# Batched experts on one core: float32 weights over SyncE's ring, cast on chip, experts in strict order

## The chip, the core and the metric

The kernel runs on one core of one Trainium2 chip. A core has engines that run side by side, each with its own instruction queue worked off in order: TensorE (PE; its weight loads are shown as PEld), VectorE (DVE), ScalarE (ACT), GpSimd (POOL) and SyncE (SP). They meet only at semaphores. Sixteen DMA engines move data between the chip's main memory (HBM) and the core's SBUF (128 partitions); a transfer is issued from an engine's queue. In this kernel transfers are issued by GpSimd, which can convert the data type on the way, and by SyncE, whose transfers here copy bytes as they are. TensorE writes its results to PSUM, from where VectorE or ScalarE copy them to SBUF.

The metric is the device time in microseconds (us). The kernel before has a median of 181.65 us over three runs (181.58 to 182.18). The profile comes from one further execution, whose first to last instruction span 180.0 us.

## What is computed

```python
# x (8, 256, 512), w1 (8, 512, 2048), w2 (8, 2048, 512), all float32
h = np.matmul(x, w1)
h = np.maximum(h, 0)
return np.matmul(h, w2).astype(np.float32)
```

Eight experts, each with a first layer (x times w1, then relu) and a second layer (h times w2). Each w1 and each w2 is 4.194 MB of float32, x and the output are 4.194 MB each. Each weight is used once, so 71.30 MB have to be read and 4.19 MB written.

## The kernel before

All matmuls run in bf16. A weight is loaded by one transfer from GpSimd's queue (`load_w1`, L67, and `load_w2`, L71) that reads float32 and lands bf16 in a buffer of 16 KB per partition; there are three buffers for each kind of weight (`WB = 3`), so a load waits until the matmuls on the buffer three experts earlier are done. On each partition the rows of a weight are one contiguous stretch of 32 KB in HBM. The w2 of the last two experts comes in two pieces.

x is taken in four groups of 1, 1, 2 and 4 experts (`GROUPS`, L34). The first two land as float32 through SyncE (L145) and are cast by ScalarE (L155, L156); the other two land as bf16 through GpSimd's queue (L65). `transpose_x` (L77) transposes 128 x 128 blocks on TensorE (L87), and VectorE (L100) or ScalarE (L98) copies them from PSUM into `xt`. For groups of more than one expert that copy writes with a stride: every second bf16 element for the group of two, every fourth for the group of four.

`first_layer` (L102) takes 64 matmuls (L110) in four quarters of 16; each quarter fills one of two PSUM buffers and is followed by a relu into `ht`, on ScalarE (L120) for quarters 0 and 2 and on VectorE (L118) for quarters 1 and 3. Quarter q reads the columns q*4 to q*4+3 of every 16 columns of w1. `second_layer` (L124) takes 32 matmuls (L130) into two PSUM tiles, which VectorE (L137) and ScalarE (L138) copy to `o_sb`.

The order on each engine is written out by hand (`manual_schedule`, L48): the calls from L144 on are issued as they stand. Experts 0 to 4 run first and second layer in turn. For experts 5, 6 and 7 the three first layers come first (L185), then the three second layers (L191). Most of the output of experts 0 to 4 is stored through GpSimd's queue behind the last weights (L189, L190), a few rows of expert 0 through SyncE (L169), and experts 5 to 7 by one last store through SyncE (L193).

Of the kernel before, what the change touches and what calls it, by code (L numbers as in the profile page):

```python
# [9 lines left out]
@with_exitstack  # L10
def kernel(
    ctx: ExitStack,
    tc: tile.TileContext,
    x: bass.AP,
    w1: bass.AP,
    w2: bass.AP,
    out: bass.AP,
):
    nc = tc.nc
    P = 128  # L20
    bf = mybir.dt.bfloat16
    f32 = mybir.dt.float32
    relu = mybir.ActivationFunctionType.Relu

    E, C, H = x.shape
    F = w1.shape[2]
    MT = C // P
    KT1 = H // P
    KT2 = F // P
    FB = 4  # L30
    WB = 3


    GROUPS = ((0, 1), (1, 1), (2, 2), (4, 4))  # L34


    w1_r = w1.rearrange("e (p kt) n -> e p kt n", p=P)
    w2_r = w2.rearrange("e (p kt) n -> e p kt n", p=P)
    out_r = out.rearrange("e (p mt) n -> p e mt n", p=P)

    const = ctx.enter_context(tc.tile_pool(name="const", bufs=1))
    wpool = ctx.enter_context(tc.tile_pool(name="weights", bufs=WB))
    hpool = ctx.enter_context(tc.tile_pool(name="hidden", bufs=3))
    ps_h = ctx.enter_context(tc.tile_pool(name="ps_h", bufs=2, space=bass.MemoryType.PSUM))
    ps_o = ctx.enter_context(tc.tile_pool(name="ps_o", bufs=4, space=bass.MemoryType.PSUM))


    ctx.enter_context(tc.manual_schedule())  # L48

    w1_sb, w2_sb, ht = {}, {}, {}  # L50
    group_of = {e: g for g, (e0, n) in enumerate(GROUPS) for e in range(e0, e0 + n)}
    x_f = const.tile([P, 2, MT, H], f32, name="x_f")
    x_b = [const.tile([P, n * MT, H], bf, name=f"x_b{g}") for g, (_, n) in enumerate(GROUPS)]
    xt = [const.tile([P, KT1, MT, n * P], bf, name=f"xt{g}") for g, (_, n) in enumerate(GROUPS)]
    o_sb = const.tile([P, E, MT, H], f32, name="out_sb")
    identity = const.tile([P, P], bf, name="identity")

    def x_rows(g):
        e0, n = GROUPS[g]
        return x[e0:e0 + n].rearrange("e c k -> (e c) k").rearrange(  # L60
            "(p j) k -> p j k", p=P
        )

    def load_x(g):
        nc.gpsimd.dma_start(x_b[g][:], x_rows(g))  # L65

    def load_w1(e):  # L67
        w1_sb[e] = wpool.tile([P, KT1, F], bf, tag="w1", name="w1_sb")
        nc.gpsimd.dma_start(w1_sb[e][:], w1_r[e])  # L69

    def load_w2(e):  # L71
        w2_sb[e] = wpool.tile([P, KT2, H], bf, tag="w2", name="w2_sb")
        cuts = {E - 2: (0, 8, 16), E - 1: (0, 9, 16)}.get(e, (0, KT2))
        for lo, hi in zip(cuts, cuts[1:]):
            nc.gpsimd.dma_start(w2_sb[e][:, lo:hi, :], w2_r[e, :, lo:hi, :])  # L75

    def transpose_x(g, blocks=None):  # L77


        n = GROUPS[g][1]  # L80
        J = n * MT
        KB = 8 // J
        for b in blocks if blocks is not None else range(KT1 // KB):
            pt = ps_o.tile([P, KB, J, P], bf, tag="ps_o", name="pt_tr")
            for i in range(KB):
                for j in range(J):
                    nc.tensor.transpose(  # L87
                        pt[:, i, j, :], x_b[g][:, j, b * KB + i::KT1], identity[:]
                    )
            for i in range(KB) if n > 1 else (slice(0, KB),):  # L90
                if n > 1:
                    src = pt[:, i].rearrange("p (l m) q -> p l m q", m=MT)
                    dst = xt[g][:, b * KB + i].rearrange("p m (q l) -> p l m q", l=n)
                    flip = b * KB + i
                else:
                    src, dst, flip = pt[:, i], xt[g][:], g
                if flip % 2:
                    nc.scalar.copy(dst, src)  # L98
                else:
                    nc.vector.tensor_copy(dst, src)  # L100

    def first_layer(e, between=()):  # L102
        g = group_of[e]
        i0 = (e - GROUPS[g][0]) * P
        ht[e] = hpool.tile([P, KT2, C], bf, tag="ht", name="ht_sb")
        for q in range(KT2 // FB):
            ph = ps_h.tile([P, FB, C], f32, tag="ps_h", name="pt_h")
            for i in range(FB):
                for kt in range(KT1):
                    nc.tensor.matmul(  # L110
                        ph[:, i, :],
                        w1_sb[e][:, kt, FB * q + i::KT2],
                        xt[g][:, kt, :, i0:i0 + P],
                        start=(kt == 0),
                        stop=(kt == KT1 - 1),
                    )
            if q % 2:
                nc.vector.tensor_relu(ht[e][:, FB * q:FB * (q + 1), :], ph[:])  # L118
            else:
                nc.scalar.activation(ht[e][:, FB * q:FB * (q + 1), :], ph[:], relu)  # L120
            if between:
                between.pop(0)()

    def second_layer(e):  # L124
        po = [
            ps_o.tile([P, H], f32, tag="ps_o", name=f"pt_o{mt}") for mt in range(MT)
        ]
        for kt in range(KT2):
            for mt in range(MT):
                nc.tensor.matmul(  # L130
                    po[mt][:],
                    ht[e][:, kt, mt * P:(mt + 1) * P],
                    w2_sb[e][:, kt, :],
                    start=(kt == 0),
                    stop=(kt == KT2 - 1),
                )
        nc.vector.tensor_copy(o_sb[:, e, 0, :], po[0][:])  # L137
        nc.scalar.copy(o_sb[:, e, 1, :], po[1][:])  # L138

    def store(e0, e1):  # L140
        nc.gpsimd.dma_start(out_r[:, e0:e1], o_sb[:, e0:e1])  # L141


    for e in (0, 1):  # L144
        nc.sync.dma_start(x_f[:, e], x_rows(e))  # L145
    load_w1(0)
    make_identity(nc, identity)
    load_w2(0)
    load_x(2)
    load_w1(1)  # L150
    load_w2(1)
    load_x(3)
    load_w1(2)
    load_w2(2)
    nc.scalar.copy(x_b[0][:], x_f[:, 0])  # L155
    nc.scalar.copy(x_b[1][:], x_f[:, 1])  # L156
    transpose_x(0)

    first_layer(0)
    load_w1(3)  # L160
    transpose_x(1)
    second_layer(0)
    load_w2(3)
    first_layer(1)
    load_w1(4)
    transpose_x(2)
    second_layer(1)
    for p in range(112, P, 4):
        nc.sync.dma_start(out_r[p:p + 4, 0], o_sb[p:p + 4, 0])  # L169
    load_w2(4)  # L170
    first_layer(2, [lambda kt=kt: transpose_x(3, [kt]) for kt in range(KT1)])
    load_w1(5)
    second_layer(2)
    first_layer(3)
    load_w1(6)
    second_layer(3)
    first_layer(4)
    load_w1(7)
    load_w2(5)
    load_w2(6)  # L180
    second_layer(4)
    load_w2(7)


    for e in (5, 6, 7):  # L185
        first_layer(e)


    store(1, 5)  # L189
    nc.gpsimd.dma_start(out_r[:112, 0], o_sb[:112, 0])  # L190
    for e in (5, 6, 7):  # L191
        second_layer(e)
    nc.sync.dma_start(out_r[:, 5:8], o_sb[:, 5:8])  # L193


# [28 lines left out]
```

## Time and profile before

| | |
|---|---|
| Median of three runs | 181.65 us |
| Span of the profiled execution | 180.0 us |
| Instructions | 1823 |
| First-layer matmuls (L110) | 512, 67.6 us busy, 31.9 us idle before them, on weights |
| Second-layer matmuls (L130) | 249 recorded, 56.2 us busy, 7.9 us idle before them |
| relu on VectorE and ScalarE (L118, L120) | 16 each, 19.7 and 16.5 us busy |
| Weight transfers issued by GpSimd (L69, L75) | 18 |
| Granted TensorE clock, mean | 0.933 |

How to read the lines that follow. The page gives, for each engine, busy time, share of the span and number of instructions; then rows of 40 digits, one for each fortieth of the span, in tenths of busy time; then the DMA queues with their packets, megabytes landed and share of the 16 engines' time. The chain of waits goes back from the last instruction to what released each step. A group row has the line, engine and operation, what it writes and reads, partitions x elements, its count, then busy us and mean ns, then the idle time of the engine before it and what ended that. A row of the timeline has start, duration, engine and line, and in square brackets the idle time before it and its releaser. A row of stretches has the busy time of each engine in it (with counts), the granted TensorE clock, the busy share of the DMA engines and GB/s. A row of DMA issues has the size of a transfer in KB and the us from issue to landing.

### The profile page before, as it was taken

How to read it: one execution, taken by the hardware profiler on the slowest of the kernel's cores; microseconds unless marked ns; L12 is line 12 of the kernel's file. 1: busy time of each engine (PE TensorE's matmuls, PEld its weight loads, DVE VectorE, ACT ScalarE, POOL GpSimd, SP SyncE). 2: the span in 40 equal slices, each digit the busy share in tenths (PEclk: the TensorE clock that was granted, in tenths of full speed). 3: DMA queues.
4: the chain of work that ended last, by engine and by line, in shares of the span. 5: the costliest groups of instructions: out<-in, count | busy, mean ns of one | idle time of the engine just before them, and what ended most of it. 6: DMA issues, size and time to landing. Idle time of an engine off the chain costs nothing.

```text
span 180.0 us, 1823 instructions
## 1 busy us (share of the span) xinstructions
PE 127.5 (71%) x825; PEld 90.1 (50%) x832; DVE 31.8 (18%) x29; ACT 31.6 (18%) x32; POOL 12.7 (7%) x28
## 2 busy tenths in 40 slices
PE   0206999059993199987869497949895876997930
PEld 0105964048840189637723395428795873442410
DVE  0100220101411018610401022010423050101010
ACT  3300240102231026612200022012222220101010
POOL 7300010100101000100100004021010000000000
PEclk9999999957999659999999789996999999999995
DMA  5998998999999999999999999999999999999996
GB/s 210 256 226 182 233 229 178 233 211 215 200 244 204 222 218 208 218 215 229 204 222 218 218 211 211 229 208 222 215 222 208 215 215 204 224 213 209 334 411 248
DMA packets 4262, 40.47 MB, mean 225 GB/s; under 512 B 416, under 2 KB 416, under 8 KB 1952
## 3 DMA queue, kind: packets, MB, share of 16 engines
q0 software_dynamic: 3536, 37.68, 95.7%
q1 hardware_dynamic: 720, 2.69, 3.9%
q8 instruction: 6, 0.10, 0.2%
HBM read 71.30 MB, written 4.19 MB: 419 GB/s over the span
## 4 chain that ended last, share of the span: by engine, by line
DMA 45%; PE 40%; another core or an unknown queue 8%; POOL 1%; issue 1%; ACT 0%; POOLq 0%
DMA w_sb<-in_w_dram 45%; PE pt_o L130 19%; PE pt_h L110 19%; PE pt_tr L87 2%; POOL w_sb L69 0%; ACT out_sb L138 0%; POOL x_b L65 0%; POOL w_sb L75 0%; POOL identity masks.py:199 0%; POOL identity masks.py:197 0%; POOLq masks.py:199 0%; POOLq L208 0%
## 5 line engine op out<-in xcount | busy, mean ns | idle before, releaser
L110 PE MATMUL pt_h<-xt,w_sb 128*128 128x256 bf16 x512 | 67.6, 299 | 31.9 <-DMA w_sb<-in_w_dram 31.9
L110 PEld LDWEIGHTS <-w_sb 128*128 128x128 bf16 x512 | 60.9, 148 | 39.1 <-DMA w_sb<-in_w_dram 35.0
L130 PE MATMUL pt_o<-w_sb,ht_sb 128*128 128x512 bf16 x249 | 56.2, 379 | 7.9 <-DMA w_sb<-in_w_dram 7.4
L130 PEld LDWEIGHTS <-ht_sb 128*128 128x128 bf16 x256 | 24.9, 98 | 37.4 <-issue 7.2
L118 DVE TENSOR_SCALAR ht_sb<-pt_h 128x1024 bf16<-128x1024 f32 x16 | 19.7, 1229 | 69.3 <-PE pt_h L110 69.3
L120 ACT ACTIVATE ht_sb<-pt_h 128x1024 bf16<-128x1024 f32 x16 | 16.5, 1031 | 72.6 <-PE pt_h L110 72.6
L138 ACT COPY out_sb<-pt_o 128x512 f32<-128x512 f32 x8 | 4.7, 586 | 58.9 <-PE pt_o L130 58.9
L137 DVE COPY out_sb<-pt_o 128x512 f32<-128x512 f32 x8 | 5.5, 692 | 53.6 <-PE pt_o L130 53.6
L69 POOL DMA_DIRECT2D w_sb<-in_w_dram x8 | 4.4, 556 | 87.4 <-PE pt_h L110 86.6
L100 DVE COPY xt<-pt_tr 128x1024 bf16<-128x1024 bf16 (+1 forms) x5 | 7.1, 1449 | 18.2 <-PE pt_tr L87 18.2
L87 PE MATMUL pt_tr<-identity,x_b 128*128 128x128 bf16 x64 | 5.6, 242 | 5.3 <-ACT x_b L155 5.3
L98 ACT COPY xt<-pt_tr 128x1024 bf16<-128x1024 bf16 (+1 forms) x5 | 7.4, 1494 | 6.9 <-PE pt_tr L87 4.3
L87 PEld LDWEIGHTS <-x_b 128*128 128x128 bf16 x64 | 4.9, 121 | 5.4 <-ACT x_b L155 5.3
L75 POOL DMA_DIRECT2D w_sb<-in_w_dram x10 | 5.4, 547 | 20.3 <-PE pt_o L130 20.3
L155 ACT CAST x_b<-x_f 128x1024 bf16<-128x1024 f32 x1 | 1.0, 1045 | 2.1 <-DMA x_f<-in_x_dram 2.1
L155 ACT ACT_TABLE_LOAD x1 | 1.3, 1283 | 0.7 <-PEq L208 0.7
L190 POOL DMA_DIRECT2D out_dram<-out_sb x1 | 0.5, 545 | 8.6 <-DMA w_sb<-in_w_dram 8.6
L65 POOL DMA_DIRECT2D x_b<-in_x_dram x2 | 1.1, 550 | 0.0
L156 ACT CAST x_b<-x_f 128x1024 bf16<-128x1024 f32 x1 | 1.0, 1047 | 0.1
L141 POOL DMA_DIRECT2D out_dram<-out_sb x1 | 0.8, 768 | 1.8 <-DMA w_sb<-in_w_dram 1.8
masks.py:199 POOL TENSOR_SCALAR_AFFINE_SELECT identity<-identity 128x128 bf16<-128x128 bf16 x1 | 0.3, 288 | 0.1
masks.py:197 POOL MEMSET identity<- 128x128 bf16 x1 | 0.2, 225 | 0.0
(4 smaller groups left out, 0.4 us busy)
## 6 DMA issues: line engine op xcount, KB each, us to landing
w_sb<-in_w_dram POOLq DMA_DIRECT2D x14, 2048.0 KB, 45.4
w_sb<-in_w_dram POOLq DMA_DIRECT2D x2, 1024.0 KB, 45.4
out_dram<-out_sb POOLq DMA_DIRECT2D x1, 2048.0 KB, 53.0
out_dram<-out_sb SPq DMA_DIRECT2D x1, 1536.0 KB, 6.0
w_sb<-in_w_dram POOLq DMA_DIRECT2D x1, 1152.0 KB, 46.6
x_f<-in_x_dram SPq DMA_DIRECT2D x2, 512.0 KB, 3.7
x_b<-in_x_dram POOLq DMA_DIRECT2D x1, 1024.0 KB, 47.9
w_sb<-in_w_dram POOLq DMA_DIRECT2D x1, 896.0 KB, 50.3
```

The source lines that it names most:

```text
L69: nc.gpsimd.dma_start(w1_sb[e][:], w1_r[e])
L75: nc.gpsimd.dma_start(w2_sb[e][:, lo:hi, :], w2_r[e, :, lo:hi, :])
L87: nc.tensor.transpose(pt[:, i, j, :], x_b[g][:, j, b * KB + i::KT1], identity[:])
L98: nc.scalar.copy(dst, src)
L100: nc.vector.tensor_copy(dst, src)
L110: nc.tensor.matmul(ph[:, i, :], w1_sb[e][:, kt, FB * q + i::KT2], xt[g][:, kt, :, i0:i0 + P], start=(kt == 0), stop=(kt == KT1 - 1),)
L118: nc.vector.tensor_relu(ht[e][:, FB * q:FB * (q + 1), :], ph[:])
L120: nc.scalar.activation(ht[e][:, FB * q:FB * (q + 1), :], ph[:], relu)
L130: nc.tensor.matmul(po[mt][:], ht[e][:, kt, mt * P:(mt + 1) * P], w2_sb[e][:, kt, :], start=(kt == 0), stop=(kt == KT2 - 1),)
L137: nc.vector.tensor_copy(o_sb[:, e, 0, :], po[0][:])
L138: nc.scalar.copy(o_sb[:, e, 1, :], po[1][:])
L155: nc.scalar.copy(x_b[0][:], x_f[:, 0])
```

## The change

All transfers are issued by SyncE, and none converts. Weights and x land as float32 in a staging pool of three buffers of 32 KB per partition (`fpool`), used in turn by x, w1 and w2. VectorE and ScalarE cast each weight into one bf16 buffer for w1 and one for w2: `cast_w1` and `cast_w2` each make four chunks, half of a chunk on each engine, 1024 elements per partition on either. The chunks of w1 are the columns of one quarter; chunks 0 and 1 are issued ahead of the first matmul, chunk q+2 behind the matmuls of quarter q and ahead of that quarter's relu. The four chunks of w2 are issued ahead of the second layer's matmuls, behind the last relu. x is cast half on VectorE and half on ScalarE. `ht` has one buffer instead of three.

The experts run in strict order, first then second layer of each. x of experts 4 to 7 is cast and transposed between expert 1 and expert 2. Only the w2 of the last expert comes in two pieces. Experts 0 to 6 are stored by one transfer behind the last load on SyncE's queue, expert 7 by a last one.

```diff
-    wpool = ctx.enter_context(tc.tile_pool(name="weights", bufs=WB))
-    hpool = ctx.enter_context(tc.tile_pool(name="hidden", bufs=3))
+    fpool = ctx.enter_context(tc.tile_pool(name="staging", bufs=3))
+    wpool = ctx.enter_context(tc.tile_pool(name="weights", bufs=1))
+    hpool = ctx.enter_context(tc.tile_pool(name="hidden", bufs=1))
...
-    def load_x(g):
-        nc.gpsimd.dma_start(x_b[g][:], x_rows(g))
+    def load_x(*groups):
+        total = sum(GROUPS[g][1] for g in groups) * MT
+        t = fpool.tile([P, total, H], f32, tag="wf", name="x_f")
+        lo = 0
+        for g in groups:
+            n = GROUPS[g][1] * MT
+            xf[g] = t[:, lo:lo + n, :]
+            nc.sync.dma_start(xf[g], x_rows(g))
+            lo += n
+
+    def cast_x(g):
+        n = GROUPS[g][1] * MT
+        nc.scalar.copy(x_b[g][:, :n // 2], xf[g][:, :n // 2])
+        nc.vector.tensor_copy(x_b[g][:, n // 2:], xf[g][:, n // 2:])
 
     def load_w1(e):
-        w1_sb[e] = wpool.tile([P, KT1, F], bf, tag="w1", name="w1_sb")
-        nc.gpsimd.dma_start(w1_sb[e][:], w1_r[e])
+        wf[e, 1] = fpool.tile([P, KT1, F], f32, tag="wf", name="w1_f")
+        nc.sync.dma_start(wf[e, 1][:], w1_r[e])
 
     def load_w2(e):
-        w2_sb[e] = wpool.tile([P, KT2, H], bf, tag="w2", name="w2_sb")
-        cuts = {E - 2: (0, 8, 16), E - 1: (0, 9, 16)}.get(e, (0, KT2))
+        wf[e, 2] = fpool.tile([P, KT2, H], f32, tag="wf", name="w2_f")
+        cuts = {E - 1: (0, 8, 16)}.get(e, (0, KT2))
         for lo, hi in zip(cuts, cuts[1:]):
-            nc.gpsimd.dma_start(w2_sb[e][:, lo:hi, :], w2_r[e, :, lo:hi, :])
+            nc.sync.dma_start(wf[e, 2][:, lo:hi, :], w2_r[e, :, lo:hi, :])
+
+    def cast_w1(e, q):
+        if q == 0:
+            w1_sb[e] = wpool.tile([P, KT1, F], bf, tag="w1", name="w1_sb")
+        dst = w1_sb[e].rearrange("p k (j i) -> p k j i", i=KT2)[:, :, :, FB * q:FB * (q + 1)]
+        src = wf[e, 1].rearrange("p k (j i) -> p k j i", i=KT2)[:, :, :, FB * q:FB * (q + 1)]
+        h = KT1 // 2
+        nc.vector.tensor_copy(dst[:, :h], src[:, :h])
+        nc.scalar.copy(dst[:, h:], src[:, h:])
+
+    def cast_w2(e, q):
+        if q == 0:
+            w2_sb[e] = wpool.tile([P, KT2, H], bf, tag="w2", name="w2_sb")
+        lo = FB * q
+        nc.vector.tensor_copy(w2_sb[e][:, lo:lo + 2], wf[e, 2][:, lo:lo + 2])
+        nc.scalar.copy(w2_sb[e][:, lo + 2:lo + 4], wf[e, 2][:, lo + 2:lo + 4])
...
     def first_layer(e, between=()):
         g = group_of[e]
         i0 = (e - GROUPS[g][0]) * P
+        cast_w1(e, 0)
+        cast_w1(e, 1)
...
+            if q + 2 < KT2 // FB:
+                cast_w1(e, q + 2)
             if q % 2:
...
     def second_layer(e):
+        for q in range(KT2 // FB):
+            cast_w2(e, q)
...
+    load_x(0, 1)
     load_w1(0)
+    load_w2(0)
     make_identity(nc, identity)
+    cast_x(0)
+    cast_x(1)
+    transpose_x(0)
+    transpose_x(1)
     load_x(2)
+
+    first_layer(0)
     load_w1(1)
+    second_layer(0)
     load_w2(1)
+    cast_x(2)
+    transpose_x(2)
     load_x(3)
...
+    for e in range(1, E):
         first_layer(e)
+        if e + 1 < E:
+            load_w1(e + 1)
+        if e + 1 == E:
+            nc.sync.dma_start(out_r[:, 0:E - 1], o_sb[:, 0:E - 1])
         second_layer(e)
+        if e == 1:
+            cast_x(3)
+            transpose_x(3)
+        if e + 1 < E:
+            load_w2(e + 1)
+    nc.sync.dma_start(out_r[:, E - 1], o_sb[:, E - 1])
```

43 lines of the change are left out of this document (1 added, 42 removed).

## The prediction

> **What bounds the kernel now.** I read the page from the top: busy shares, the slices, the queues, the chain.
>
> ```profile
> span 180.0 us, 1823 instructions
> PE 127.5 (71%) x825; PEld 90.1 (50%) x832; DVE 31.8 (18%) x29; ACT 31.6 (18%) x32; POOL 12.7 (7%) x28
> ...
> DMA  5998998999999999999999999999999999999996
> ...
> q0 software_dynamic: 3536, 37.68, 95.7%
> q1 hardware_dynamic: 720, 2.69, 3.9%
> ...
> HBM read 71.30 MB, written 4.19 MB: 419 GB/s over the span
> ...
> DMA 45%; PE 40%; another core or an unknown queue 8%; POOL 1%; issue 1%; ACT 0%; POOLq 0%
> ```
>
> The 16 DMA engines are busy in nearly every slice; TensorE is not (71%), VectorE and ScalarE are at 18%. The chain is weights and the matmuls that wait for them. 71.30 MB are read, although only about half as many bytes land, because GpSimd's queue converts to bf16 on the way. Next, the middle of the timeline, and stretches of the span (the last column is GB/s landed or stored, the one before it the busy share of the DMA engines).
>
> ```profile
> 81.95 7.22 PE L110 MATMUL pt_h<-xt,w_sb 128*128 128x256 bf16 x64 [1.48 <-DMA w_sb<-in_w_dram]
> ...
> 91.65 7.07 PE L130 MATMUL pt_o<-w_sb,ht_sb 128*128 128x512 bf16 x31 [2.48 <-DMA w_sb<-in_w_dram]
> ...
> 98.54 0.69 DVE L137 COPY out_sb<-pt_o 128x512 f32<-128x512 f32 x1 [8.11 <-PE pt_o L130]
> 98.75 0.59 ACT L138 COPY out_sb<-pt_o 128x512 f32<-128x512 f32 x1 [10.27 <-PE pt_o L130]
> ...
> 101.32 8.71 PE L110 MATMUL pt_h<-xt,w_sb 128*128 128x256 bf16 x64 [2.60 <-DMA w_sb<-in_w_dram]
> ...
> 140.11 7.21 PE L110 MATMUL pt_h<-xt,w_sb 128*128 128x256 bf16 x64 [2.50 <-DMA w_sb<-in_w_dram]
> ```
>
> ```profile
> 2.50:4.50 2.00, 0.00 (x0) 0.00 (x0) 0.00 (x0) 0.34 (x1) 2.00 (x4) 1.00 1.00 393
> 8.00:165.00 157.00, 119.20 (x786) 86.33 (x793) 30.45 (x27) 27.67 (x28) 7.67 (x14) 0.93 1.02 216
> 169.00:173.00 4.00, 3.24 (x15) 1.27 (x13) 0.69 (x1) 0.52 (x1) 0.00 (x0) 1.00 1.03 425
> 174.50:178.00 3.50, 0.00 (x0) 0.00 (x0) 0.00 (x0) 0.00 (x0) 0.00 (x0) 0.74 1.00 406
> ...
> 30.00:60.00 30.00, 19.27 (x120) 12.92 (x119) 5.09 (x6) 4.57 (x6) 1.59 (x3) 0.89 1.03 218
> ...
> 178.00:178.50 0.50, 0.00 (x0) 0.00 (x0) 0.00 (x0) 0.00 (x0) 0.00 (x0) 0.50 0.39 156
> ```
>
> Every stage of TensorE starts on a weight landing, and the landings are 9.7 us apart (81.95, 91.65, 101.32). One load reads 4.194 MB: 432 GB/s of float32, the same as twice the 216 landed over 157 us. The kernel is bound by bytes read; compute has room inside each period. The tail:
>
> ```profile
> 165.00 4.06 PE L130 MATMUL pt_o<-w_sb,ht_sb 128*128 128x512 bf16 x18 [1.24 <-DMA w_sb<-in_w_dram]
> 169.26 3.18 PE L130 MATMUL pt_o<-w_sb,ht_sb 128*128 128x512 bf16 x14 [0.20 <-DMA w_sb<-in_w_dram]
> ...
> 172.48 0.59 ACT L138 COPY out_sb<-pt_o 128x512 f32<-128x512 f32 x1 [8.09 <-PE pt_o L130]
> 173.09 0.41 SPq L193 DMA_DIRECT2D out_dram<-out_sb  x1
> ```
>
> ```profile
> out_dram<-out_sb SPq DMA_DIRECT2D x1, 1536.0 KB, 6.0
> ```
>
> The last weights land at 169.2. Behind them stand 14 matmuls, copies to 173.07 and a store of three experts that lands at 173.09 + 6.0 = 179.1, with 0.9 to the span's end.
>
> **The change: the stream.** The bytes read stay the same; what changes is who moves them. Start: SyncE issues its first transfer at 0.74 and bytes move from 1.75, as after.
>
> ```profile
> 0.74 0.88 SPq L145 DMA_DIRECT2D x_f<-in_x_dram  x2
> ...
> 1.75:2.00 0.25, 0.00 (x0) 0.00 (x0) 0.00 (x0) 0.25 (x1) 0.25 (x2) 1.00 1.38 197
> ```
>
> No row has a float32 weight on SyncE's ring. Its own rows are 393 (x at the start, beside the first weights) and 406 GB/s (the final store alone); its 720 packets of 2.69 MB are 4 KB rows plus completions. The upper end is 436, twice the 218 of the stretch from 30 to 60. The rows differ in packet size: 4096 B on one of 16 engines is 161 ns at 406 GB/s and 152 at 432, so 10 ns a packet; the weights' rows are 32 KB (1214 ns at 432), where 10 ns are 0.8%. I take 429, nearest to the row of the same bytes, and keep 406 and 436. 71.30 MB / 429 = 166.2, so the stream ends at 167.95. From the store, whose bytes flow until about 178.4 and which lands at 179.1, I take 0.7 from last byte to landing.
>
> [...]
>
> **Does the ring run dry?** A load of 4 MB waits until the casts of three loads earlier are done. The casts of a w1 are done about 6 us after it lands; the load that reuses its slot comes up in the stream one further load (9.8 us) after the next one has ended, so some 19 us later. A w2's casts end about 14 us after the w1 ahead of it. At least 10 us of cover: I cost this wait at 0. SyncE's queue holds loads and, behind all of them, two stores, so a blocked load delays only later loads.
>
> **The change: the casts.** Per weight four chunks, each 1024 elements per partition on VectorE and 1024 on ScalarE.
>
> ```profile
> L155 ACT CAST x_b<-x_f 128x1024 bf16<-128x1024 f32 x1 | 1.0, 1045 | 2.1 <-DMA x_f<-in_x_dram 2.1
> ...
> L118 DVE TENSOR_SCALAR ht_sb<-pt_h 128x1024 bf16<-128x1024 f32 x16 | 19.7, 1229 | 69.3 <-PE pt_h L110 69.3
> L120 ACT ACTIVATE ht_sb<-pt_h 128x1024 bf16<-128x1024 f32 x16 | 16.5, 1031 | 72.6 <-PE pt_h L110 72.6
> ...
> L98 ACT COPY xt<-pt_tr 128x512 bf16<-128x512 bf16 x2 | 1.4, 734 | 2.6 <-DVE xt L100 2.6
> ```
>
> ```profile
> 24.72 1.01 ACT L98 COPY xt<-pt_tr 128x1024 bf16<-128x1024 bf16 x1 [1.17 <-PE pt_tr L87]
> ...
> 65.79 1.06 PE L87 MATMUL pt_tr<-identity,x_b 128*128 128x128 bf16 x8
> ...
> 66.89 2.57 DVE L100 COPY xt<-pt_tr 128x1024 bf16<-128x1024 bf16 x1 [10.97 <-PE pt_tr L87]
> ...
> 69.19 2.55 ACT L98 COPY xt<-pt_tr 128x1024 bf16<-128x1024 bf16 x1 [2.13 <-PE pt_tr L87]
> ```
>
> ScalarE: 1.05, the same operation. VectorE has no cast: between 0.69 (its 512-element copy, were it twice as fast) and 1.23 (its 1024-element relu); I take 1.05. The w2 chunks are contiguous. The w1 chunks take four elements of every sixteen. Strided copies are in the trace: group 2 writes every 4 bytes and needs 0.73 for 512, group 3 writes every 8 bytes and needs 2.55 for 1024. So a w1 chunk lies between 1.05 and 2.55. Its runs of 8 bytes put four elements into 16 bytes, as group 2's do: I take 1.05 and leave 2.55 to a rival.
>
> [...]
>
> Sixteen weights times four chunks is 64 x 1.05 = 67 us more on each engine, about 100 us in all. None of it counts as such; what counts is the serial chain of one expert, since all is now in strict order. From w1's landing: chunk 0 on both engines 1.1; 64 matmuls 7.22 (later chunks run beside them: a quarter of the matmuls takes 1.8, and on ScalarE three casts and a relu end 4.2 after landing); relu of the last quarter, which stands ahead of w2's casts on VectorE, 1.28; chunk 0 of w2 1.1 (w2 has landed by then); 32 matmuls and copies 7.69 (91.65 to 99.34). Sum **18.4 us**, against a stream of 2 x 4.194 / 429 = **19.56** an expert. The next w1's casts stand behind the copies, so this does not overlap; it fits, with 1.2 to spare. Transposing the last four experts' x stands between experts 1 and 2: casts 2.1, transposes 1.06 and two copies of 2.55 on each engine. By the same sums expert 2 starts about 4 us late, and 1.2 an expert makes that good by expert 6.
>
> **The end.** w1 of expert 7 lands at 167.95 - 9.78 + 0.7 = 158.9. The chain ends at 177.3. The store of experts 0 to 6 (3.67 MB, 9.0 at 406) runs from 167.95 to 177.0, hidden. The last store: 6.0 - 1.573/0.406 = 2.1 fixed, and 0.524 MB / 0.406 = 1.3, so 3.4: landing 180.7, end 181.6. TensorE's clock: after 2.60 idle one first layer took 8.71, after 2.50 another 7.21. Here the gaps are 2.4 (relu and cast) and, once the lag is gone, about 3, so the last expert may pay 1.5; half of it, 0.75. Span 182.4. The profiled execution before has 180.0 and the median is 181.65, so 1.65 more: **184.0 us**, 1.3% slower. Set against the tail before: last weights 0.55 earlier, 8.6 instead of 3.9 from there to the end of the copies, 2.6 less for the smaller store.
>
> **Rivals.**
> *Faster.* The stream runs at its 436 and the casts are cheap. For it: SyncE's ring needs no issue by GpSimd, and the middle of the trace touches 436. Against: 406 on that ring. Stream end 165.3, w1 of expert 7 at 156.4, chain with VectorE at 0.69 for a w2 chunk 18.05, warm clock: 156.4 + 18.05 + 3.4 + 0.9 + 1.65 = 180.4. It decides from about 434 GB/s on.
> *Slow ring.* The weights move at the 406 of that ring's rows whatever the packet. 71.30/0.406 = 175.6, 9.4 more: 193.4.
> *The compute chain outgrows the stream.* If a w1 chunk takes 2.55, ScalarE needs 2.55 x 4 + 1.03 before the last quarter, and an expert takes 11.2 + 1.8 + 1.28 + 1.1 + 7.69 = 23.1, 3.5 above the stream. Experts 2 to 7 with 4 us of lag: 4 + 5 x 3.5 = 21.5 late, and 4.7 more in the last: about 209. If instead a cast waits for the matmuls that read the same buffer (one buffer a layer), 3 us more an expert give about 199. For it: one buffer, strict order, the 2.55 rows. Against: each chunk is a part of its own. It decides from 19.56 an expert, a w1 chunk of about 1.6.
> *It does not do what it says*: transfers that stay on GpSimd's queue would show as q0; nothing in the diff leaves any.
>
> **Chances.** Forecast 0.54 (181.5 to 187, from 432 with a warm clock to 425 with cold starts), faster 0.14, slow ring 0.15, compute chain 0.17. The range leaves out most of the compute chain and little else: 180 to 193.5. Within 0.3% (what a measurement of this kernel can't tell from no change) is 181.1 to 182.2: 0.12, from the forecast's lower edge. Faster 0.17, with a few hundredths of that edge; slower 0.71.
>
> **What would show it.** q0 gone, q1 with some 75 MB; about 9.8 us between landings, and GB/s near 429 in the middle; casts of 1.05 on ScalarE, and at L100 the same 2.55; SyncE's waits without gaps in the DMA slices; last weights at about 168.7, the copies at 177.3. The prediction is wrong if a middle window shows under 415 or over 434, if a w1 cast passes 1.6, or if the DMA slices show holes.

## The result, and the profile after

The changed kernel takes 183.91 us (median of four runs, 183.61 to 184.39), the kernel before 181.69 beside it: a ratio of 1.012, 95% interval 1.0098 to 1.0141. It is slower by 2.2 us, where 184.0 was forecast. A run more than 1.5% above the fastest of its kernel is left out of ratios and medians below; this concerns a single run, of the delay in expert 1. The changed kernel's profiled execution spans 182.0 us, against 180.0 before.

The page of the changed kernel: span, busy times, DMA slices, queues, bytes, chain.

```profile
span 182.0 us, 1994 instructions
...
PE 129.7 (71%) x832; PEld 90.0 (49%) x832; DVE 73.3 (40%) x97; ACT 94.8 (52%) x98; POOL 0.7 (0%) x6
...
DMA  5999999999999999999999999999999999999983
...
q1 hardware_dynamic: 4080, 75.50, 97.2%
...
HBM read 71.30 MB, written 4.19 MB: 415 GB/s over the span
```

GpSimd's queue q0 is gone; everything goes through q1. The same bytes are read. VectorE and ScalarE work 41 and 63 us more, TensorE as before. The DMA slices have no hole until the last two. Stretches of the changed kernel (last column GB/s, before it the DMA share):

```profile
8.00:165.00 157.00, 116.69 (x751) 81.76 (x752) 66.26 (x87) 85.29 (x89) 0.00 (x0) 0.93 1.00 430
...
175.00:177.00 2.00, 2.00 (x11) 0.90 (x10) 0.00 (x0) 0.00 (x0) 0.00 (x0) 1.00 0.83 340
177.00:179.00 2.00, 0.79 (x4) 0.18 (x2) 0.69 (x1) 0.59 (x1) 0.00 (x0) 1.00 0.20 82
179.00:181.00 2.00, 0.00 (x0) 0.00 (x0) 0.00 (x0) 0.00 (x0) 0.00 (x0) 0.81 0.65 262
```

430 GB/s of float32 in the middle, where twice 216 were read before: the stream is as fast on SyncE's ring. New is the hole from 177 to 179: the large store is out, and the last one cannot start, because expert 7 is still being computed. The changed kernel's groups of casts and relus:

```profile
L149 DVE TENSOR_SCALAR ht_sb<-pt_h 128x1024 bf16<-128x1024 f32 x16 | 19.6, 1225 | 44.2 <-PE pt_h L139 21.0
L95 ACT CAST w_sb<-w_f 128x1024 bf16<-128x1024 f32 x32 | 32.0, 1051 | 9.8 <-DMA w_f<-in_w_dram 9.8
L102 ACT CAST w_sb<-w_f 128x1024 bf16<-128x1024 f32 x32 | 31.2, 1043 | 5.1 <-DMA w_f<-in_w_dram 5.1
...
L94 DVE CAST w_sb<-w_f 128x1024 bf16<-128x1024 f32 x32 | 20.0, 689 | 12.1 <-DMA w_f<-in_w_dram 11.7
```

A strided w1 chunk (L95) costs ScalarE what a contiguous w2 chunk (L102) does; VectorE needs 0.69 for either. TensorE's timeline of the changed kernel (start, duration, idle time before it):

```profile
86.05 7.45 PE L139 MATMUL pt_h<-xt,w_sb 128*128 128x256 bf16 x64 [1.17 <-DVE w_sb L94]
95.41 7.07 PE L163 MATMUL pt_o<-w_sb,ht_sb 128*128 128x512 bf16 x32 [1.92 <-DVE w_sb L101]
103.65 7.45 PE L139 MATMUL pt_h<-xt,w_sb 128*128 128x256 bf16 x64 [1.17 <-DVE w_sb L94]
...
122.61 8.63 PE L139 MATMUL pt_h<-xt,w_sb 128*128 128x256 bf16 x64 [2.54 <-DVE w_sb L94]
...
142.04 9.00 PE L139 MATMUL pt_h<-xt,w_sb 128*128 128x256 bf16 x64 [1.82 <-DVE w_sb L94]
...
161.48 7.32 PE L139 MATMUL pt_h<-xt,w_sb 128*128 128x256 bf16 x64 [1.46 <-DVE w_sb L94]
170.72 7.07 PE L163 MATMUL pt_o<-w_sb,ht_sb 128*128 128x512 bf16 x32 [1.92 <-DVE w_sb L101]
```

From 86.05 to 103.65 an expert takes 17.6 us: here it still makes good the late start behind the transposes of x. From 122.61 on the steps are 19.4, the stream's two landings. The end, from the timelines of ScalarE and of SyncE and from the DMA issues:

```profile
170.40 1.99 ACT L102 CAST w_sb<-w_f 128x1024 bf16<-128x1024 f32 x2 [0.40 <-DMA w_f<-in_w_dram]
177.83 0.59 ACT L171 COPY out_sb<-pt_o 128x512 f32<-128x512 f32 x1 [5.44 <-PE pt_o L163]
```

```profile
178.44 0.35 SPq L203 DMA_DIRECT2D out_dram<-out_sb  x1
```

```profile
out_dram<-out_sb SPq DMA_DIRECT2D x1, 3584.0 KB, 18.3
...
out_dram<-out_sb SPq DMA_DIRECT2D x1, 512.0 KB, 2.6
```

| | before | after | difference |
|---|---|---|---|
| Last weights landed | 169.2 | 170.4 | +1.2 |
| From there to the end of the copies | 3.9 | 8.0 | +4.1 |
| From there to the end of the span | 6.9 | 3.6 | -3.3 |
| Span | 180.0 | 182.0 | +2.0 |

### The profile page after: what moved, and what is told of

Its sections match the earlier page's. It is cut to its first block, busy times and chain, and to the rows that moved or that the text cites. A ratio compares the mean times of both kernels' runs of the same rounds, so it can differ in the third digit from the quotient of the medians.

```text
span 182.0 us, 1994 instructions
## 1 busy us (share of the span) xinstructions
PE 129.7 (71%) x832; PEld 90.0 (49%) x832; DVE 73.3 (40%) x97; ACT 94.8 (52%) x98; POOL 0.7 (0%) x6
## 5 line engine op out<-in xcount | busy, mean ns | idle before, releaser
L139 PEld LDWEIGHTS <-w_sb 128*128 128x128 bf16 x512 | 60.0, 148 | 31.9 <-DVE w_sb L94 26.2
L163 PE MATMUL pt_o<-w_sb,ht_sb 128*128 128x512 bf16 x256 | 56.5, 379 | 15.3 <-DVE w_sb L101 15.3
L163 PEld LDWEIGHTS <-ht_sb 128*128 128x128 bf16 x256 | 25.0, 98 | 45.1 <-issue 16.7
L95 ACT CAST w_sb<-w_f 128x1024 bf16<-128x1024 f32 x32 | 32.0, 1051 | 9.8 <-DMA w_f<-in_w_dram 9.8
L102 ACT CAST w_sb<-w_f 128x1024 bf16<-128x1024 f32 x32 | 31.2, 1043 | 5.1 <-DMA w_f<-in_w_dram 5.1
L94 DVE CAST w_sb<-w_f 128x1024 bf16<-128x1024 f32 x32 | 20.0, 689 | 12.1 <-DMA w_f<-in_w_dram 11.7
L101 DVE CAST w_sb<-w_f 128x1024 bf16<-128x1024 f32 x32 | 19.9, 686 | 0.0
L114 PE MATMUL pt_tr<-identity,x_b 128*128 128x128 bf16 x64 | 6.2, 272 | 9.1 <-ACT x_b L75 9.1
L75 ACT CAST x_b<-x_f 128x512 bf16<-128x512 f32 (+2 forms) x4 | 4.2, 1047 | 2.7 <-DMA x_f<-in_x_dram 2.7
L76 DVE CAST x_b<-x_f 128x512 bf16<-128x512 f32 (+2 forms) x4 | 2.8, 688 | 4.9 <-DMA x_f<-in_x_dram 4.9
## 6 DMA issues: line engine op xcount, KB each, us to landing
x_f<-in_x_dram SPq DMA_DIRECT2D x1, 2048.0 KB, 16.7
```

The costliest lines, as they stand in the source:

```text
L75: nc.scalar.copy(x_b[g][:, :n // 2], xf[g][:, :n // 2])
L94: nc.vector.tensor_copy(dst[:, :h], src[:, :h])
L95: nc.scalar.copy(dst[:, h:], src[:, h:])
L101: nc.vector.tensor_copy(w2_sb[e][:, lo:lo + 2], wf[e, 2][:, lo:lo + 2])
L102: nc.scalar.copy(w2_sb[e][:, lo + 2:lo + 4], wf[e, 2][:, lo + 2:lo + 4])
L114: nc.tensor.transpose(pt[:, i, j, :], x_b[g][:, j, b * KB + i::KT1], identity[:])
```

## The experiments

The theory put to the test: the stream is no slower, the middle of the kernel is hidden under it, and the serial chain of the last expert (casts, first layer, relu, cast, second layer, copies, store) sets the end. Rivals: the ring is slower; every expert's chain counts; the strict order by itself is the loss; the bytes on the ring set the end whatever the chain does.

**A delay in the last expert, and the same in expert 1.**

```diff
     def cast_w2(e, q):
...
         nc.scalar.copy(w2_sb[e][:, lo + 2:lo + 4], wf[e, 2][:, lo + 2:lo + 4])
+        if e == 7 and q == 0:      # e == 1 in the other
+            for _ in range(4):
+                nc.vector.tensor_copy(w2_sb[e][:, 0:2], wf[e, 2][:, 0:2])
```

> Four more casts of the same 1024 elements of w2 on VectorE, 0.69 us each, 2.76 us in all, ahead of the last expert's second layer. Theory (the serial chain of the last expert sets the end: its copies end at 178.42, only then is the last store issued): the whole 2.76 comes through, span about 184.7, time about 186.6. Rival (the end is set by the bytes on SyncE's ring, the large store lands at 178.97 anyway): at most 0.6 comes through, time at most 184.5.

Measured: 189.5 us, ratio 1.0431 (1.0372 to 1.0489). Not 2.8 but 5 to 6 us come through: the medians are 5.6 apart. The rival's 184.5 is out. TensorE at the end of this run:

```profile
162.04 9.00 PE L142 MATMUL pt_h<-xt,w_sb 128*128 128x256 bf16 x64 [1.84 <-DVE w_sb L94]
175.86 8.75 PE L166 MATMUL pt_o<-w_sb,ht_sb 128*128 128x512 bf16 x32 [4.83 <-DVE w_sb L105]
```

The four casts widen the gap from 1.92 to 4.83, and behind it the second layer takes 8.75 instead of 7.07. The granted clock, the share of its full speed that TensorE got, was 0.50 from 177 to 179 us and 0.82 from 179 to 181 in it, and 1.00 all through the changed kernel's last second layer. This execution also has a first layer of 9.00 in its last expert (granted clock 0.76 from 160 to 167 us), where the changed kernel has 7.32 (1.00); so the 2.76, twice 1.7 and a start of expert 7 that is 0.56 later make up nearly all of the 6.8 by which its span is longer.

> The same four casts ahead of expert 1's second layer. Theory (between landings there is 1 to 2 us of room for each expert, and a lag is made good before the last one): no change, 183.5 to 184.3. Rival (every expert's chain of casts and matmuls adds up to the time, the stream waits for it): about 186.6.

Measured: 185.66 us (184.06, 185.66 and 186.01; a fourth run took 187.73), ratio 1.020 (1.0146 to 1.0253): between the two, and scattered. The profiled execution, of span 182.3, shows the delay being made good:

```profile
54.41 9.10 PE L166 MATMUL pt_o<-w_sb,ht_sb 128*128 128x512 bf16 x32 [4.83 <-DVE w_sb L105]
...
71.97 0.51 PE L142 MATMUL pt_h<-xt,w_sb 128*128 128x256 bf16 x2 [4.01 <-DVE w_sb L94]
```

```profile
161.67 7.45 PE L142 MATMUL pt_h<-xt,w_sb 128*128 128x256 bf16 x64 [1.17 <-DVE w_sb L94]
```

Expert 2 starts at 71.97, 6.0 later than in the changed kernel (66.01), expert 7 at 161.67, 0.2 later; the gap of 1.17 ahead of it is that of the chain, so not even expert 7 waited for data. The second layer behind the delay took 9.10 instead of 7.07, so what had to be made good was nearer 5 us than 2.8. A lag is made good at up to 1.8 us an expert (19.4 less 17.6), and here all of that room was used up. The expectation of no change holds for this execution and not for the median; the middle of the kernel hides such a delay only as far as this room goes. That the longer executions lost more of TensorE's clock on the way, with no room left for it, was not seen, as only one execution is profiled, but their mean granted clocks fit: 0.951 at 184.06 us, 0.944 at 185.66, 0.941 at 186.01, 0.936 at 187.73.

**The order alone.** The kernel before, with its converting transfers, but in the changed kernel's order at the end, and with the loads in the order of use.

```diff
+    load_w2(5)
...
+    load_w2(6)
...
-    load_w2(5)
-    load_w2(6)
...
-    for e in (5, 6, 7):
-        first_layer(e)
-    store(1, 5)
-    nc.gpsimd.dma_start(out_r[:112, 0], o_sb[:112, 0])
-    for e in (5, 6, 7):
-        second_layer(e)
-    nc.sync.dma_start(out_r[:, 5:8], o_sb[:, 5:8])
+    for e in (5, 6):
+        first_layer(e)
+        second_layer(e)
+    first_layer(7)
+    store(1, 7)
+    nc.gpsimd.dma_start(out_r[:112, 0], o_sb[:112, 0])
+    second_layer(7)
+    nc.sync.dma_start(out_r[:, 7], o_sb[:, 7])
```

> The kernel before, with GpSimd's converting transfers, but all eight experts in strict order, loads in the order of use, experts 0 to 6 stored behind the last load and expert 7 alone at the end. Theory (it is the casts in the last expert's chain together with the order that cost; without casts the chain is 1.1 + 0.7 shorter, and the last second layer starts before its last piece lands): span 179.9 to 180.7, time 181.5 to 182.4. Rival (the strict order by itself is the loss): 183.5 or more.

Measured: 181.79 us, ratio 1.0014 (1.0004 to 1.0023), span 179.6. The order alone costs 0.25 us, not 2. TensorE's and SyncE's timelines of this run:

```profile
159.05 8.80 PE L110 MATMUL pt_h<-xt,w_sb 128*128 128x256 bf16 x64 [5.33 <-DMA w_sb<-in_w_dram]
167.68 7.07 PE L130 MATMUL pt_o<-w_sb,ht_sb 128*128 128x512 bf16 x32
```

```profile
175.40 0.36 SPq L190 DMA_DIRECT2D out_dram<-out_sb  x1
```

Expert 7 needs no cast: its second layer follows the first without a gap, although that first layer took 8.80, with a granted clock of 0.83 from 160 to 167 us. The last store goes out at 175.40, 3.0 ahead of the changed kernel's.

**Reordering the last two experts** of the changed kernel (first, first, second, second; `ht` with two buffers, w1 of expert 7 loaded ahead of w2 of expert 6; to make room, the bf16 x of experts 0 and 1 shares a buffer with that of experts 4 to 7). The end of the order on each engine:

```diff
...
+    first_layer(E - 2)
+    load_w2(E - 2)
+    first_layer(E - 1)
+    load_w2(E - 1)
+    nc.sync.dma_start(out_r[:, 0:E - 2], o_sb[:, 0:E - 2])
+    second_layer(E - 2)
+    second_layer(E - 1)
+    nc.sync.dma_start(out_r[:, E - 2:], o_sb[:, E - 2:])
```

> The changed kernel, with the last two experts as first, first, second, second layer; w1 of expert 7 is loaded ahead of w2 of expert 6, ht has two buffers, and the last store takes experts 6 and 7. Theory (2 us of the end are a hole in the DMA stream between the large store and the last one): the last weights land at 170.4 as before, the copies end at about 175.5, the last store follows the large one without a hole, span about 180.3, time about 182.1. Rival (the last weights land later because SyncE's ring is slower, and that is the loss): no more than 0.5 is won, 183.4 or more.

Measured: 186.32 us, ratio 1.0241 (1.0199 to 1.0284). A miss: slower than the changed kernel.

```profile
152.74 8.99 PE L140 MATMUL pt_h<-xt,w_sb 128*128 128x256 bf16 x64 [2.38 <-DVE w_sb L95]
163.64 7.07 PE L164 MATMUL pt_o<-w_sb,ht_sb 128*128 128x512 bf16 x32 [1.92 <-DVE w_sb L102]
171.88 7.07 PE L164 MATMUL pt_o<-w_sb,ht_sb 128*128 128x512 bf16 x32 [1.17 <-DVE w_sb L102]
```

```profile
161.61 3.88 ACT L103 CAST w_sb<-w_f 128x1024 bf16<-128x1024 f32 x4 [0.57 <-DMA w_f<-in_w_dram]
```

```profile
177.00:179.00 2.00, 1.95 (x10) 0.69 (x7) 0.23 (x1) 0.02 (x1) 0.00 (x0) 1.00 0.13 51
```

My sum started the last chain at the last landing. But now two second layers stand behind it: the w2 of expert 6 lands only at about 161.6 (ScalarE's cast of it starts then), and from 163.64 on TensorE works without a wait for data, 2 x 7.07 with copies and a cast between. The copies end at 179.6, and the store after them is twice as large. The hole in the stream is there again: a DMA share of 0.13 from 177 to 179. The first layer of 8.99 is 1.7 longer than the one ahead of it (7.33); not all of that counts, since w2 of expert 6 was not there before 161.6. This run does not speak for the ring rival: from 163.64 on nothing waited for the ring.

**The changed kernel again, and its last gap shortened.**

```diff
...
+            if e == E - 1 and q == 3:
+                cast_w2(e, 0)
+                cast_w2(e, 1)
+                nc.vector.tensor_relu(ht[e][:, FB * q:FB * q + 2, :], ph[:, 0:2])
+                nc.scalar.activation(ht[e][:, FB * q + 2:FB * (q + 1), :], ph[:, 2:4], relu)
...
-        for q in range(KT2 // FB):
+        for q in range(2 if e == E - 1 else 0, KT2 // FB):
             cast_w2(e, q)
...
```

> The changed kernel once more, as it is, beside the others of this set. Theory: 183.5 to 184.5. Rival (this kernel's time depends on whether TensorE's clock drops in gaps of 1.8 to 2.6 us, so it scatters more than the kernel before): single times spread over more than 1.5, up to 186.

> The changed kernel; in the last expert alone, the first two chunks of w2 are cast ahead of the last relu, and that relu is split over VectorE and ScalarE, so that the gap between its layers shrinks from 1.92 to about 0.75. Theory (the last expert's chain sets the end): the copies end 1.2 earlier, at about 177.2, the last store then follows the large one with little hole: 1.0 less than the changed kernel beside it. Rival (the end is set by the last weights at 170.4 and the bytes of the ring): within 0.3 of it.

Measured: the changed kernel 183.38 us (183.12 to 183.52; ratio 1.0098, 1.0079 to 1.0117), so the scatter feared in its rival did not appear here; the shortened one 182.69 (182.18 to 183.59; ratio 1.0068, 1.0044 to 1.0091). Of the 1.0 expected, 0.7 came by the medians and about 0.5 by the ratios, whose intervals overlap. Four of its nine runs lie at 183.5 or just above; the other five, at 182.2 to 182.7, are below every one of the twelve times of the changed kernel on record (183.12 to 184.39). The profiled execution is one of the four (183.50), so its timelines show the shorter chain, not the gain in time:

```profile
162.08 7.33 PE L139 MATMUL pt_h<-xt,w_sb 128*128 128x256 bf16 x64 [1.45 <-DVE w_sb L94]
169.25 7.07 PE L168 MATMUL pt_o<-w_sb,ht_sb 128*128 128x512 bf16 x31
```

```profile
176.97 0.35 SPq L208 DMA_DIRECT2D out_dram<-out_sb  x1
```

The gap is gone; the second layer starts 7.2 after the first instead of 9.2, and the store 1.5 earlier than in the changed kernel, although expert 7 starts 0.6 later. That store then takes 3.9 us to land instead of 2.6, since the large one is still ahead of it on the ring (DMA share 0.70 from 177 to 178 us, where the changed kernel has 0.37). In this execution a second layer of 8.75 (expert 5) and a first layer of 9.00 (expert 6) stand ahead of the late start of expert 7; that these two long layers (others in it take 7.07 and 7.33) took the gain away is likely, not shown. In the five shorter executions, taking time out of the last chain took time out of the kernel.

**The two rings alone.** All matmuls, casts and relus are left out; a copy of two elements on VectorE stands behind each landing.

```diff
...
+    for e in range(E):
+        load_w1(e)
+        load_w2(e)
+        nc.vector.tensor_copy(x_b[3][:, 0, 4 * e:4 * e + 2], wf[e, 1][:, KT1 - 1, F - 2:])
+        nc.vector.tensor_copy(x_b[3][:, 0, 4 * e + 2:4 * e + 4], wf[e, 2][:, KT2 - 1, H - 2:])
...
```

> All matmuls, casts and relus left out: only the loads of the changed kernel on SyncE's ring in its order, three buffers, with a copy of two elements on VectorE behind each landing, and the stores of a zeroed output. Theory (both rings read the same bytes at the same rate): last weights at 168.5 to 169.7, landings 9.7 to 9.8 apart. Rival (SyncE's ring is slower): last weights at 170.4 or later, landings of 9.85 or more.

> The same loads alone, but issued by GpSimd and converted to bf16 on the way; matmuls, casts and relus are left out here too. Theory: last weights within 1 us of the run on SyncE's ring. Rival (SyncE's ring is slower): 1.5 us or more ahead of it.

VectorE's timeline on SyncE's ring, then on GpSimd's (start of the copy behind a landing):

```profile
16.32 0.17 DVE L180 CAST x_b<-w_f 128x2 bf16<-128x2 f32 x1 [6.91 <-DMA w_f<-in_w_dram]
...
120.83 0.17 DVE L180 CAST x_b<-w_f 128x2 bf16<-128x2 f32 x1 [9.54 <-DMA w_f<-in_w_dram]
130.56 0.17 DVE L181 CAST x_b<-w_f 128x2 bf16<-128x2 f32 x1 [9.57 <-DMA w_f<-in_w_dram]
...
169.52 0.17 DVE L181 CAST x_b<-w_f 128x2 bf16<-128x2 f32 x1 [9.65 <-DMA w_f<-in_w_dram]
```

```profile
122.73 0.17 DVE L181 COPY x_b<-w_f 128x2 bf16<-128x2 bf16 x1 [9.52 <-DMA w_f<-in_w_dram]
132.45 0.17 DVE L180 COPY x_b<-w_f 128x2 bf16<-128x2 bf16 x1 [9.54 <-DMA w_f<-in_w_dram]
```

Landings are 9.7 apart on both (on GpSimd's only after its stores were through; until 84 us they were 11 apart): SyncE's ring carries float32 at 4.194 / 9.71 = 432 GB/s in 32 KB rows. The last weights are there at 169.5 with no compute at all, and at 170.4, 169.8 and 170.2 in the three profiled executions of the changed kernel: beside the compute the ring loses 0.3 to 0.9. Which part of the compute costs it was not tested. One run each, of 182.06 and 184.26 us. The second does not answer the question of the last landing, since its stores, on SyncE, ran in the middle of its loads. The first landing of a w1 does differ: 16.32 here, and 16.32, 16.20 and 15.59 in the three executions of the changed kernel (15.3 to 16.7 over all profiled runs on this ring); in the kernel before, its first layer starts at

```profile
15.08 5.12 PE L110 MATMUL pt_h<-xt,w_sb 128*128 128x256 bf16 x27 [8.78 <-DMA w_sb<-in_w_dram]
```

1.2 earlier than 16.32 for the same bytes. At the last landing 0.3 of this is left (169.5 against 169.2). Why the first one takes longer, and why it varies, stays open.

**TensorE's clock.** The delay again, the delay with its gap filled by matmuls that nobody reads, and such matmuls in the gaps of experts 2 to 7 of the changed kernel. The code is that of the filled gap; in the last run it is `keep_busy(8)` from expert 2 on, and `keep_busy(5)` behind the second layers of experts 2 to 6.

```diff
...
+    def keep_busy(n):
+        junk = ps_o.tile([P, H], f32, tag="ps_o", name="junk")
+        for _ in range(n):
+            nc.tensor.matmul(junk[:], identity[:], xt[3][:, 0, 0, :], start=True, stop=True)
...
+        if e == E - 1:
+            keep_busy(20)
```

> The changed kernel as it is, to stand beside the three others of this set: 183.1 to 184.4.

> The four extra casts ahead of the last expert's second layer once more. The first run of it took 4 us more than the 2.76 of the casts; its trace has the last second layer at 8.75 behind an idle gap of 4.83, where the changed kernel has 7.07 behind 1.92. Theory (the delay opens a gap in which TensorE's clock drops): 3 or more above the casts' price again, 188 to 190.6, last second layer 8.5 to 9.1. Rival (something else of that chip or run): 186.0 to 187.

> The same, with 20 matmuls on data that is there, into a PSUM tile that nobody reads, in that gap (about 4.3 us of work in 4.83). Theory (the clock): the last second layer is back at 7.07, and the time 1.5 to 1.9 below the run without them. Rival (the clock has no part): no change, within 0.3 of it.

> The changed kernel with 8 such unread matmuls between the layers of experts 2 to 7 (1.7 us in a gap of 1.92) and 5 behind the second layers of experts 2 to 6. Theory (the clock drops in gaps of about 2 us and more in some executions and costs 1.5 each time; whatever reaches expert 7 shows in the end): first layers of experts 3 to 7 all at 7.3 to 7.5, time 0 to 0.8 below the changed kernel beside it. Rival (the chain has no room for more matmuls): slower by 0.5 or more.

Measured: the changed kernel 183.70 us (ratio 1.0117, 1.0098 to 1.0136); with the delay 188.80 (1.0395, 1.0345 to 1.0445; two runs at 187.95, with mean granted clocks of 0.936 and 0.945, two at 189.65, both with 0.924); with the gap filled 186.87 (1.0300, 1.0272 to 1.0327); with all gaps filled 183.66 (1.0125, 1.0097 to 1.0152). TensorE in the run with the delay, then in the one with the gap filled:

```profile
173.26 0.42 PE L166 MATMUL pt_o<-w_sb,ht_sb 128*128 128x512 bf16 x1 [4.83 <-DVE w_sb L105]
173.90 8.12 PE L166 MATMUL pt_o<-w_sb,ht_sb 128*128 128x512 bf16 x30 [0.22 <-issue]
```

```profile
169.21 4.26 PE L161 MATMUL junk<-xt,identity 128*128 128x512 bf16 x19
173.98 7.07 PE L173 MATMUL pt_o<-w_sb,ht_sb 128*128 128x512 bf16 x31 [0.51 <-DVE w_sb L105]
```

More work, 1.9 us less time: the second layer is back at 7.07, and 186.87 is 3.2 above the changed kernel, close to the price of the four casts. Without the fill the last second layer took 8.76 (173.26 to 182.02), as in the first run with the delay, where 8.75 went with granted clocks of 0.50 and 0.82. So the surplus of the delay was the clock, seen in this pair by these lengths alone. In the changed kernel itself, filling the gaps wins nothing. Every first layer from expert 3 on takes 7.3 to 7.5 and every second layer 7.07, but the plain run beside it has first layers just as short and only one slow second layer (8.75, of expert 5), so this pair does not show what the fill does for the clock. Nor was there time to win ahead of expert 7: in both runs it waits for its w1. ScalarE in the run with the gaps filled:

```profile
160.48 2.95 ACT L95 CAST w_sb<-w_f 128x1024 bf16<-128x1024 f32 x3 [1.25 <-DMA w_f<-in_w_dram]
```

## Why the prediction was right, point by point

*The stream keeps its pace on SyncE's ring.* Right: 430 GB/s in the middle and 432 alone, where 429 was taken; the slow-ring rival (406 whatever the packet) is out.

*When the last weights land.* Mis-sized: 168.65 predicted, 170.4 measured. The failing term is the start rather than the rate: stream from 1.75 and 0.7 from last byte to landing would put the first w1 at 14.67; it came at 16.32, 1.65 later. From there on the loads alone took 153.2 us where 429 GB/s would take 154.0, so 0.8 came back, and 0.9 were lost beside the compute: together the 1.75. The two other profiled executions of the changed kernel share it out otherwise (first w1 at 16.20 and 15.59, last weights at 169.8 and 170.2), and why the start is late stays open.

*The ring does not run dry.* Right: loads alone are at most 0.9 ahead of the whole kernel at the end, and the w1 of expert 7, for one, was issued at 135.47, some 15 us before the load ahead of it landed (cast from 150.98 on).

*The casts.* Right in both choices: 1.05 on ScalarE for contiguous and strided chunks, so the 2.55 of group 3's copies did not carry over to runs of four elements. Counting the elements in 16 bytes was the author's estimate; no run varies it. VectorE was taken at 1.05 and needs 0.69, the lower bound.

*The chain of an expert fits under the stream.* Right: 18.4 predicted, 17.6 measured, under 19.4. Expert 2 was to start about 4 us late, by the prediction's sums at 66.3; it did at 66.0, and at 68.4 and 66.7 in the two other profiled executions. That the first of these fits so well is luck in part, since its w1 landed later than the sum has it (about 62.6 instead of 61.1, an estimate from the landings before and after it) and the lag was smaller. The lag was to be gone by expert 6 and is gone by expert 5 here, where TensorE again waits for w1 (2.54 at 122.61). The compute-chain rival is out.

*The end.* The mechanism was right and is shown by the delay in the last expert and by its shortened gap; the order alone, without casts, costs 0.25. Of its terms, the chain behind the last landing was 8.6 predicted, 8.0 measured; the last store with the end of the span 4.3 predicted, 3.6 measured; half a drop of the clock, 0.75, was added, and in the profiled execution none fell in the last expert (7.32 and 7.07, granted clock 1.00). These three are 2.1 too much, the late landing 1.75 too little. That 184.0 met 183.91 to a tenth is luck: errors that cancel.

*The faster rival* had the stream at 436 GB/s. Alone, SyncE's ring took 9.71 us a load, 432.

## What to carry to other kernels

In this kernel, bound by bytes, work moved onto idle engines was hidden in the middle as far as each period had room for it (1.8 us an expert), and was paid for in the chain behind the last landing (8.0 us instead of 3.9). In another such kernel, work out that chain, and what the transfer queue has left to do meanwhile. A delay there was paid in full here (3.2 us for 2.76 of casts with the gap filled), and more where TensorE's clock dropped behind the gap (5.1 and 5.6 us, with a second layer of 8.75 instead of 7.07). A delay in the middle is not always free: four casts in expert 1 used up all the room that the experts behind it had, and two of three executions ended 1.7 to 2.1 later for it. No version tried here beats the kernel before: its transfers have no hole, and with SyncE's ring the loads and stores alone took 182.06 in the one run of them.

## What the runs showed of the hardware that was not expected

The granted clock does not follow the length of the last idle gap alone: a first layer took 9.00 behind 1.82 us of idle time and 7.32 behind 2.66, in two executions of the same kernel (granted clock 0.81 and 1.00). The second of these, from another execution of the changed kernel:

```profile
160.87 7.32 PE L139 MATMUL pt_h<-xt,w_sb 128*128 128x256 bf16 x64 [2.66 <-DVE w_sb L94]
```

VectorE cast 1024 float32 elements to bf16 in 0.69 us, 1.5 times as fast as ScalarE (1.05), also in runs of four elements at a stride of sixteen.
